# FoX attention moved from the mixer stage to the Strassen pairs, with GLA and HGRN2 side by side

## The chip, the cores and the metric

The kernel runs on one core of one Trainium2 chip. The metric is device time in microseconds (us). Before the change three runs took 2003.84, 2007.07 and 2007.81 us; their median is 2007.07 us. TensorE (PE) multiplies matrices, VectorE (DVE), ScalarE (ACT) and GpSimd (POOL) work element by element, and SyncE (SP) issues most DMAs.

## The reference

One layer of a hybrid decoder, for a prompt of 1024 tokens and for 8 samples of 4 tokens, with the same weights; width 1024, float32. Three mixers stand beside each other and are fed by one input projection:

```
def _mixer(xn, ...):
    z = xn @ w_in
    (gq, gk, gv, glr, gr, fq, fk, fv, ff, hq, hf, hi, hg, ga, gb, gc) = jnp.split(z, ...)
    o_a, gla_s = _gated_linear_scan(gq * GLA_DK ** -0.5, gk, gv, log_a, gla_s0)      # GLA, 4 heads, 64 x 128
    o_a = _rms_norm(o_a, gla_norm_g) * silu(gr)
    logf = log_sigmoid(ff + fox_bf)
    o_b = fox_attend(fq, fk, fv, logf)                                              # FoX, 4 heads of 128
    o_c, hg_s = _gated_linear_scan(silu(hq), one_minus_f, hi, log_f, hg_s0)         # HGRN2, 4 heads, 128 x 128
    o_c = _rms_norm(o_c, hg_norm_g) * silu(hg)
    merged = sigmoid(ga) * (o_a @ w_branch_a) + sigmoid(gb) * (o_b @ w_branch_b) + sigmoid(gc) * (o_c @ w_branch_c)
    return merged @ w_out, gla_s, hg_s, fk_h, fv_h, logf
# FoX, one block of 128 queries of the prompt; c = cumsum(logf)
    s = einsum('bqhd,bkhd->bhqk', qi, k) * scale
    p = softmax(where(kpos <= qpos, s + c[t] - c[s], -inf));  o = p @ v
# FoX of the samples reads 1024 past tokens through a page table, and the 4 new ones
# layer: x = x + mixer;  h = rms_norm(x);  x = x + (silu(h @ w_gate) * (h @ w_up)) @ w_down;  final rms_norm
```

## The kernel before

**Numbers and tiles.** Activations lie feature by feature: a tile has 128 features on the partitions and 1056 columns, the 1024 prompt tokens and the 32 sample tokens. Each float32 operand is split into a high and a low part (`split`, L210: ACT writes the high part, DVE subtracts it), and a product is three matmuls: high by high, high by low, low by high. An ordinary tile of a projection (`gemm`, L115) goes in three chunks of 352 columns; a chunk of the input projection is 8 x 3 matmuls (L136).

**Strassen pairs.** Most of the input projection goes in 22 pairs of output tiles (`in_pairs` L550, `pair_run` L1662). A pair is seven Strassen products (P1, P5, P6, P2, P7, P3, P4), each for two column parts of 264, each with 4 x 3 matmuls (L1693): 168 matmuls. A result is added to an output tile by DVE (L1700) or copied there by ACT (L1702). The seven weight operands are four blocks of the loaded weights and sums of them: `pair_sums` (L1625) computes the sums on DVE, `pair_split` splits each. The weights of the next pair are prepared while the last four products of this pair run; a ring of four buffers of two operands each holds them. At a pair's end `post` (L561) multiplies both outputs by the norm's factor, one on DVE, one on GpSimd (L568), applies the gates' sigmoid where there is one, and sends the tiles to DRAM.

**Mixer stage.** From 535 to 1110 us run 16 single tiles of the branch gates and the branch products (24 jobs). Between chunks, `gemm` calls `pump`, which takes one step of a generator from each of several queues: `bg` holds the four FoX heads, `bg2` FoX's sample part, `bg3` the two GLA pairs and then the four HGRN2 heads, `bgs` the sample parts of the scans. The generators issue their own matmuls among those of the tiles, in the order in which the pump meets them, and every engine runs its instructions in that order. PSUM has eight banks: seven for the pairs; in the mixer stage three for tiles (`pg`) and five for the generators (`pm`).

**FoX.** `fox_head` (L722) sums the forget gates (the scan L1146), turns the values to token order (L707), and then goes through eight query blocks: scores (L780), a DVE reduction that subtracts the bias and takes the maximum, the exponential on ACT, the normalisation on DVE (L800), transposes of the weights on PE (L746), their copy out on ACT (L748) and the product with the values (L759). Transposes and products of a block come two blocks behind its scores (`DEPTH` is 2). `fox_sample` (L811) reads 64 pages of keys and values, 0.5 MB each, with matmuls of four columns of samples (L927).

**Scans and branches.** Each scan of GLA and HGRN2 is in two halves: L1068 to L1072 scale on DVE and POOL, L1085 scores, L1106 states, L1132 and L1134 outputs. After the first eight branch tiles `any_range` (L1350) reads whether a gate's range was too wide for the fast form; the branch (L1354) with the slow form is not taken here. The branch products come in the order GLA, HGRN2, FoX.

Of the kernel before, what the change touches and what calls it, by code (L numbers as in the profile page):

```python
# [18 lines left out]
NP = 1024  # L19
# [18 lines left out]
NA, NBU, NH, NAT = 10, 8, 8, 4  # L38
KVRING = 3
LAST = ((0, 400), (400, 800), (800, NT))  # L40
SAMPLE_WITH = 2
AHEAD = 7
DEPTH = 2
# [47 lines left out]
class Body:  # L91
    def __init__(self, nc, tc, A, O):
        self.nc, self.tc, self.A, self.O = nc, tc, A, O
        self.bg, self.bgs, self.bg2, self.bg3 = [], [], [], []
# [20 lines left out]
    def gemm(self, job, nxt):  # L115
# [13 lines left out]
        for c in range(0 if job.tiles_first else NCW):  # L129
# [14 lines left out]
            self.pump(self.bg3, self.bgs, self.bg, self.bg2)  # L144
# [43 lines left out]
    def pump(self, *qs):  # L188

        if self.cold:  # L190
            return
        for q in qs or (self.bg, self.bgs, self.bg2, self.bg3):
            if q and next(q[0], "end") == "end":
                q.pop(0)
# [76 lines left out]
    def run(self):  # L271
# [21 lines left out]
        self.st = [pe.tile([128, 512], F32, name=f"st{i}") for i in range(3)]  # L293
# [5 lines left out]
    def all_jobs(self):  # L299
# [7 lines left out]
        yield Job(None, 0, None, None, run=self.in_pairs, ahead=lambda: self.pair_ahead(lambda n: self.A["winp"][n], len(PAIRS) // 2))  # L307
# [4 lines left out]
    def phase_m(self):  # L312
# [15 lines left out]
        self.bg += [self.fox_head(h) for h in range(4) if ("fv", h) not in TILES[4:]]  # L328
        self.bg3 += [self.gla_pair(p) for p in range(2)] + [self.hgrn_head(h) for h in range(4)]
# [9 lines left out]
    def constants(self):  # L339
# [21 lines left out]
        self.cmask = const("cmask", [128, 128])  # L361
        self.nmask = const("nmask", [128, NS])
        self.bmask = const("bmask", [128, NB, NS])
        self.tmask = const("tmask", [NS, NB])
        self.pts = const("pt", [1, NB * NPG], I32)
        self.ptr = const("ptr", [128, NPG], I32)
        self.hcol = const("hcol", [128, 1])
# [4 lines left out]

        self.fox_q1 = cp.tile([128, 4, NS], F32, name="fox_q1")
        self.fox_ks = cp.tile([128, 4, NS], F32, name="fox_ks")
        self.fox_vs = cp.tile([NS, 4, 128], F32, name="fox_vs")
        self.fox_cn = cp.tile([128, NS], F32, name="fox_cn")
# [173 lines left out]
    def in_pairs(self, job, nxt):  # L550
# [4 lines left out]
        def phase():  # L555
            self.close("s")
            p = self.open("p", "right", reuse_waits="tile")
            self.u = Slots(p, 6, [128, NT], F32, "pu")
            return [(p.tile([128, 1024], F32R, name=f"rh{i}"), p.tile([128, 1024], F32R, name=f"rl{i}")) for i in range(2)]

        def post(n, y):  # L561
            name = PAIRS[2 * n][0]
            e = nc.vector, nc.gpsimd
            for i in range(2):
                if name == "gq":
                    nc.vector.scalar_tensor_tensor(y[i], y[i], 0.125, self.r1, ALU.mult, ALU.mult)
                else:
                    e[i].tensor_tensor(y[i], y[i], self.r1, ALU.mult)  # L568
            if name in ("gr", "hq", "hg"):
                g = [self.u.get(), self.u.get()]  # L570
                for i in range(2):
                    self.sig = nc.scalar.activation(g[i], y[i], AF.Sigmoid)
                for i in range(2):
                    e[i].tensor_tensor(y[i], y[i], g[i], ALU.mult)
                self.u.put(*g)
            for i in range(2):
                self.keep(*PAIRS[2 * n + i], y[i])
            self.u.put(*y)

        def hook(n, k):  # L580
# [3 lines left out]
            if k == 0:  # L584
# [3 lines left out]
            elif k == 2:  # L588
# [5 lines left out]
        self.pair_run(nxt, phase, post, hook)  # L594
# [38 lines left out]
    def mixer_jobs(self):  # L633
        for n, h in TILES[4:]:
            yield self.store(n, h, (lambda h=h: self.bg.append(self.fox_head(h))) if n == "fv" else None)
# [63 lines left out]
    def tok_major(self, vT, vs):  # L699

        nc = self.nc
        v = self.u.get()
# [18 lines left out]

    def fox_head(self, h):  # L722
        nc = self.nc
        yield from self.room(5)
        vT, q, k = [self.fetch(n, h) for n in ("fv", "fq", "fk")]
        cb = self.u.get()
        nc.sync.dma_start(cb, self.lf_dram[h:h + 1, :].to_broadcast([128, NT]))
        yield
        v, vu = self.tok_major(vT, None)
        self.u.put(vT)  # L730

        self.sums(cb, NP)
        yield
        if h == SAMPLE_WITH:
            self.bg2.append(self.fox_sample())
        yield from self.room(4)
        o = self.u.get()
        psos = {}

        def turned(i, x):  # L740

            for j0 in range(0, i + 1, 4):
                nb = min(4, i + 1 - j0)
                pt = self.pm.get()
                for j in range(nb):
                    nc.tensor.transpose(pt[:, j * 128:(j + 1) * 128], x[:, (j0 + j) * 128:(j0 + j + 1) * 128], self.ident)  # L746
                P = self.hf.get()
                nc.scalar.activation(P[:, :nb * 128], pt[:, :nb * 128], AF.Copy)  # L748
                self.pm.put(pt)
                if j0 + nb == i + 1:  # L750
                    self.u.put(x)
                yield j0, nb, P

        def values(i, j0, nb, P):
            if i % 4 == 0 and j0 == 0:
                psos[0] = self.pm.get()
            pso = psos[0]
            for j in range(nb):
                nc.tensor.matmul(pso[:, (i % 4) * 128:(i % 4 + 1) * 128], v[:, j0 + j, :], P[:, j * 128:(j + 1) * 128],  # L759
                                 start=j0 + j == 0, stop=j0 + j == i)  # L760
            self.hf.put(P)
            if i % 4 == 3 and j0 + nb == i + 1:
                nc.vector.tensor_copy(o[:, (i - 3) * 128:(i + 1) * 128], pso)
                self.pm.put(pso)

        prev = []
        for i in range(8):
            n = (i + 1) * 128
            x = self.u.get()
            cbd = self.sp.tile([128, 128], F32, tag="cbd", name="cbd", bufs=2)  # L770
            nc.gpsimd.tensor_tensor(cbd, cb[:, n - 128:n], self.cmask, ALU.add)
            m = self.sp.tile([128, 4], F32, tag="fm", name="fm", bufs=4)
            init = -3.0e38
            nm = 0
            tp = turned(*prev.pop(0)) if len(prev) == DEPTH else iter(())
            for s0 in range(0, n, 512):
                part = next(tp, None)
                w = min(512, n - s0)
                ps = self.pm.get()
                nc.tensor.matmul(ps[:, :w], q[:, i * 128:(i + 1) * 128], k[:, s0:s0 + w], start=True, stop=True)  # L780
                d0 = i * 128 - s0
                full = w if d0 >= w else d0
                if full > 0:
                    nc.vector.tensor_tensor_reduce(x[:, s0:s0 + full], ps[:, :full], cb[:, s0:s0 + full], 1.0, init,
                                                   ALU.subtract, ALU.max, m[:, nm:nm + 1])
                    init = m[:, nm:nm + 1]
                    nm += 1
                if d0 < w:
# [1298 lines left out]
```

## Time and profile before

| | |
|---|---|
| median of 3 runs | 2007.07 us |
| profiled execution | 2003.84 us |
| its span | 2002.0 us |
| PE busy | 1936.3 us, 97% |
| DVE busy | 1372.3 us, 69% |
| ACT busy | 808.6 us, 40% |
| POOL busy | 456.6 us, 23% |

The span is the profiled execution from its first to its last instruction. The stages stand one behind the other: norm and first tiles to 90 us, pairs of the input projection to 535 us, mixers and branches to 1110 us, output projection to 1280 us, the FFN's pairs behind it. The granted clock in the profile's rows is a share of TensorE's full clock: 1.00 is its level of 2.4 GHz, 0.50 that of 1.2 GHz. The profile's matmul rows are pipelined: the cost of one in a row of many is the distance of the starts, not its own duration.

### The profile page before, as it was taken

The page shows a single profiled execution, that of the slowest core. Times are in us where ns is not written, and L with a number is a line of the kernel's source. Part 1 is how long each engine was busy: PE and PEld are TensorE (multiplying, and loading weights), DVE is VectorE, ACT ScalarE, POOL GpSimd, SP SyncE. Part 2 cuts the span into 40 slices and gives each one's busy share as a digit, 9 for nine tenths or more (in the row PEclk, how much of TensorE's full clock was granted, in tenths as well). Part 3 has the DMA queues.
Part 4 walks back from the last instruction along what each step waited for, and adds up shares of the span by engine and source line. Part 5 has one row for each costly group of instructions (what it writes and reads, how often), then busy time and mean ns, then how long its engine had stood idle before and what let it go on. Part 6 is the DMA issues. An engine that isn't in the chain of part 4 may idle for free. (4 is left out here: it accounts for less than half of the span.)

```text
span 2002.0 us, 36377 instructions
## 1 busy us (share of the span) xinstructions
PE 1936.3 (97%) x14590; PEld 1816.3 (91%) x14590; DVE 1372.3 (69%) x2279; ACT 808.6 (40%) x1448; POOL 456.6 (23%) x269
## 2 busy tenths in 40 slices
PE   8899999999989999999999999999999999999997
PEld 6899999999976777787788999999999999999996
DVE  8866577666476767667744555878777777667965
ACT  5433343333244435355343333543333333323435
POOL 5110122211121322112201631133222322111004
PEclk9999999999988989999999999999999999999999
DMA  3343222333434226676775443221222122333212
GB/s 132 108 158 132 99 106 97 107 107 119 135 139 152 96 98 217 213 225 220 231 252 198 160 156 119 75 75 67 101 80 75 65 83 75 133 113 121 84 59 87
DMA packets 88630, 253.65 MB, mean 127 GB/s; under 512 B 13634, under 2 KB 18690, under 8 KB 88450
## 3 DMA queue, kind: packets, MB, share of 16 engines
q1 hardware_dynamic: 86898, 250.02, 36.8%
q8 instruction: 117, 1.92, 0.4%
q10 hardware_dynamic: 1296, 0.67, 0.1%
q14 instruction: 63, 0.52, 0.1%
q0 software_dynamic: 256, 0.52, 0.1%
HBM read 183.80 MB, written 67.37 MB: 125 GB/s over the span
## 5 line engine op out<-in xcount | busy, mean ns | idle before, releaser
L136 PE MATMUL pg<-x,wh 128*128 128x352 f32 x1692 | 434.0, 336 | 11.5 <-DVE ub L629 6.7
L136 PEld LDWEIGHTS pg<-x,wh 128*128 128x128 f32 x1692 | 298.1, 192 | 37.0 <-issue 26.2
L1693 PE MATMUL pg<-x,wh 128*128 128x264 f32 x1632 | 308.6, 285 | 3.4 <-DVE du L1700 2.3
L136 PE MATMUL pg<-x,wl 128*128 128x352 f32 x846 | 280.6, 332 | 0.1
L1693 PE MATMUL pg<-x,rh 128*128 128x264 f32 x1424 | 267.3, 285 | 2.2 <-DVE fu L1700 2.2
L1693 PEld LDWEIGHTS pg<-x,wh 128*128 128x128 f32 x1632 | 253.3, 188 | 5.7 <-DVE du L1700 2.5
L1693 PE MATMUL pg<-x,wl 128*128 128x264 f32 x816 | 231.7, 284 | 2.3 <-DVE wl L215 2.3
L1693 PEld LDWEIGHTS pg<-x,rh 128*128 128x128 f32 x1424 | 221.7, 189 | 2.5 <-DVE fu L1700 2.4
L1693 PE MATMUL pg<-x,rl 128*128 128x264 f32 x712 | 202.8, 285 | 0.0
L136 PEld LDWEIGHTS pg<-x,wl 128*128 128x128 f32 x846 | 162.4, 192 | 4.2 <-issue 3.0
L1693 PEld LDWEIGHTS pg<-x,wl 128*128 128x128 f32 x816 | 153.4, 188 | 2.5 <-DVE wl L215 2.5
L568 POOL TENSOR_TENSOR pu<-pu,r 128x1056 f32<-128x1056 f32 x21 | 59.2, 2818 | 378.6 <-ACT pu L1702 378.6
L1693 PEld LDWEIGHTS pg<-x,rl 128*128 128x128 f32 x712 | 134.6, 189 | 0.0
L214 ACT ACTIVATE wh<-wf 128x512 fp32r<-128x512 f32 (+2 forms) x110 | 68.1, 619 | 158.9 <-PE pg L1693 120.2
L215 DVE TENSOR_TENSOR wl<-wf,wh 128x512 fp32r<-128x512 f32 (+2 forms) x110 | 85.6, 778 | 46.7 <-ACT wh L214 45.2
L1728 POOL TENSOR_TENSOR fu<-fu,r 128x1056 f32<-128x1056 f32 x22 | 67.2, 3057 | 215.9 <-ACT fu L1702 202.7
L107 ACT ACTIVATE wh<-wf 128x1024 fp32r<-128x1024 f32 (+2 forms) x60 | 51.3, 854 | 146.8 <-PE pg L136 105.8
L1630 DVE TENSOR_TENSOR st<-wf 128x512 f32<-128x512 f32 x44 | 87.2, 1982 | 32.8 <-DMA wf<-in_winp 19.0
L1693 PE MATMUL pg<-pr,wh 128*128 128x264 f32 x544 | 103.1, 288 | 3.7 <-ACT pu L1702 3.7
L1700 DVE TENSOR_TENSOR pu<-pu,pg 128x264 f32<-128x264 f32 x132 | 56.4, 428 | 72.2 <-PE pg L1693 71.9
L215 DVE TENSOR_TENSOR rl<-wf,rh 128x512 fp32r<-128x512 f32 x85 | 69.8, 822 | 47.7 <-ACT rh L214 46.8
L214 ACT ACTIVATE rh<-wf 128x512 fp32r<-128x512 f32 x85 | 53.5, 631 | 112.2 <-PE pg L1693 83.7
(519 smaller groups left out, 4594.6 us busy)
## 6 DMA issues: line engine op xcount, KB each, us to landing
z_dram<-pu SPq DMA_DIRECT2D x44, 528.0 KB
wf<-in_winp SPq DMA_DIRECT2D x44, 512.0 KB
wf<-in_wgu SPq DMA_DIRECT2D x44, 512.0 KB
u<-z_dram SPq DMA_DIRECT2D x36, 528.0 KB
ub<-z_dram SPq DMA_DIRECT2D x28, 528.0 KB
wf<-in_win SPq DMA_DIRECT2D x19, 512.0 KB
a_dram<-fu SPq DMA_DIRECT2D x18, 528.0 KB
du<-a_dram SPq DMA_DIRECT2D x14, 528.0 KB
```

The costliest lines, as they stand in the source:

```text
L107: nc.scalar.activation(wh[:, :n], wf[:, :n], AF.Copy)
L136: nc.tensor.matmul(ps[:m, :CW], a[:, k, :], b[:, sl], start=n == 0, stop=n == 3 * job.kt - 1)
L214: nc.scalar.activation(h, x, AF.Copy)
L215: (eng or nc.vector).tensor_tensor(l, x, h.bitcast(F32), ALU.subtract)
L568: e[i].tensor_tensor(y[i], y[i], self.r1, ALU.mult)
L1630: nc.vector.tensor_tensor(s[0], a2[:, x], a2[:, y], ALU.add)
L1693: nc.tensor.matmul(ps, a[:, w], b, start=first and m == 0, stop=m == 3 * K - 1, skip_group_check=not first)
L1700: nc.vector.tensor_tensor(out, out, ps, ALU.add)
L1728: TT = lambda e, o, x, y, op=ALU.mult: e.tensor_tensor(o, x, y, op)
```

## The change

**FoX goes to the pairs.** `in_pairs` opens FoX's own buffers (`fox_open`) once the norm's are closed; PSUM is split into six banks for the pairs and two for FoX. After each product of a column part, that is after every 12 matmuls, `pair_run` calls `beside`, which takes one step of the queue `bg`: first the four heads, then the sample. `fox_head` is written anew as 33 steps with a fixed order: in a step of the blocks with more than 512 keys stand a score matmul of one block and the transposes or value products of the block before. `fox_sample` gives way twice per page instead of once. A head joins the queue when its value tile is stored.

**Weights of the pairs roll.** In place of a whole pair of weights ahead, a table (`ROLL`) says which split and which sum is done behind each product; three raw buffers turn, five quarters of split weights are held instead of eight. `post` becomes a generator that is advanced one step behind each product. The order of the pairs changes: the tiles with a sigmoid come last.

**GLA beside HGRN2.** Two queues, `bg3` for the two GLA pairs and `bg4` for the four HGRN2 heads, are both pumped between the gate tiles. In a scan the second half's first matmuls are issued later, among the first half's.

**Branches.** Their order is FoX, GLA, HGRN2. The slow form, not taken, now saves and restores the partial result.

```
-NA, NBU, NH, NAT = 10, 8, 8, 4
+NA, NBU, NH, NAT = 10, 8, 10, 4
-PAIRS += [(n, t) for n, c in (("gq", 2), ("gk", 2), ("gv", 4), ("gr", 4), ("hq", 4), ("hf", 4), ("hg", 4), ("hi", 4)) for t in range(c)]
-PAIRS += GATES[24 - 2 * NGP:]
+PAIRS += [(n, t) for n, c in (("gq", 2), ("gk", 2), ("gv", 4), ("hf", 4), ("hi", 4)) for t in range(c)]
+PAIRS += GATES[24 - 2 * NGP:20]
+PAIRS += [(n, t) for n in ("gr", "hq", "hg") for t in range(4)]
+PAIRS += GATES[20:]
...
                 if k == 3 and job.kt == KD:
-                    self.pump(self.bg, self.bg3, self.bgs, self.bg2)
+                    self.pump(self.bg3, self.bgs)
...
-            self.pump(self.bg3, self.bgs, self.bg, self.bg2)
+            self.pump(self.bg4, self.bgs, *(() if job.kt == KD else (self.bg3,)))
...
-            self.u = Slots(p, 6, [128, NT], F32, "pu")
-            return [(p.tile([128, 1024], F32R, name=f"rh{i}"), p.tile([128, 1024], F32R, name=f"rl{i}")) for i in range(2)]
+            self.u = Slots(p, 5, [128, NT], F32, "pu")
+            ring = p.tile([128, 512], F32R, name="rh"), p.tile([128, 512], F32R, name="rl")
+            self.fox_open(p)
+            self.bg.append(self.fox_head(0))
+            return [ring]
...
-        self.pair_run(nxt, phase, post, hook)
+        self.pair_run(nxt, phase, post, hook, beside=lambda: self.pump(self.bg))
+        self.drain(self.bg)
...
+    def fox_open(self, p):
+        self.fa = Slots(p, 5, [128, NT], F32, "fa")
+        self.fp = Slots(p, 3, [128, 512], F32, "fp")
+        self.fb = Slots(p, 6, [128, 128], F32, "fb")
+        self.fs = Slots(p, 4, [128, 8], F32, "fs")
...
+        for i in range(9):
+            S = list(blocks[i][0]) if i < 8 else []
+            TV = list(blocks[i - 1][2]) if i else []
+            steps = max(len(S), len(TV))
+            if i < 8 and steps == len(S):
+                steps += 1
+            for j in range(steps):
+                if stored:
+                    stored.pop(0)()
+                if pend:
+                    pend[0]()
+                if TV and j % 2:
+                    TV.pop(0)()
+                if S:
+                    S.pop(0)()
+                    new = None if S else blocks[i][1]
+                else:
+                    new = None
+                if TV and j % 2 == 0:
+                    TV.pop(0)()
+                if pend:
+                    pend[1]()
+                pend = new
                 yield
...
-        order = [(bi, f) for bi in (0, 2, 1) for f in range(8)]
+        order = [(bi, f) for bi in (1, 0, 2) for f in range(8)]
...
+    ROLL = {3: (1, "P1", "S1"), 4: (1, "P5", "S2"), 5: (1, "P6", "S3"), 6: (1, "P2", "S4"), 0: (0, "P7"), 1: (0, "P3"), 2: (0, "P4")}
...
-        self.banks(7)
+        self.banks(6 if beside else 7)
...
+                    if beside:
+                        beside()
                 has.add(self.READS[name])
+                if pend and next(pend[0], "end") == "end":
+                    pend.pop()
+                if rolling:
+                    m, *names = self.ROLL[k]
+                    self.roll(n + m, *names)
```

In `fox_head` the pair `pend` holds the exponential and the normalisation of a block; `S` are its scores, `TV` the transposes and value products of the block before.

On PE before, in the mixer stage, FoX's transposes (L746), value products (L759) and scores (L780) stand a few tile matmuls (L136) apart:

```order
L780 MATMUL pg_97<-ub_5427,ub_5421 128x256
L136 MATMUL pg_98<-x_75,wh_71 128x352
L136 MATMUL pg_98<-x_76,wh_71 128x352
L746 MATMUL pg_94<-c_ident,ub_5426 128x128 x4
...
L136 MATMUL pg_98<-x_79,wh_71 128x352
L759 MATMUL pg_91<-h_5407,u_5398 128x128 x4
...
L746 MATMUL pg_95<-c_ident,ub_5422 128x128 x4
L780 MATMUL pg_94<-ub_5427,ub_5421 128x512
L759 MATMUL pg_96<-h_5412,u_5398 128x128 x4
```

On PE of the change, in the pairs, a step of FoX (scores L801, transposes L832, value products L845) stands behind every 12 pair matmuls (L1813), and FoX's tiles have two banks in turn, here `pg_93` and `pg_94`:

```order
L801 MATMUL pg_94<-fa_825,fb_830 128x512
L832 MATMUL pg_93<-f_ident,fa_824 128x128 x4
L1813 MATMUL pg_96<-x_77,wh_71 128x264
...
L845 MATMUL pg_94<-fp_827,fa_822 128x128 x4
L801 MATMUL pg_93<-fa_825,fb_830 128x256
L1813 MATMUL pg_97<-x_77,wh_71 128x264
...
L832 MATMUL pg_93<-f_ident,fa_824 128x128
L1813 MATMUL pg_98<-pr_219,wh_72 128x264
...
L845 MATMUL pg_94<-fp_828,fa_822 128x128
```

The FoX matmuls stand now at even distances, and the scores' second part takes the bank that the transposes have just left.

On DVE before, in a pair, stand the evacuations (L1700), the splits (L215), the post product (L568) and the sums (L1630, L1631):

```order
L215 TENSOR_TENSOR rl_821<-st_237,rh_820 128x512
L1700 TENSOR_TENSOR pu_818<-pu_818,pg_92 128x264
L1700 TENSOR_TENSOR pu_818<-pu_818,pg_96 128x264
L215 TENSOR_TENSOR rl_821<-wf_70,rh_820 128x512
L568 TENSOR_TENSOR pu_818<-pu_818,r_261 128x1056
L1630 TENSOR_TENSOR st_235<-wf_70 128x512
L1631 TENSOR_TENSOR st_236<-st_235,wf_69 128x512
```

On DVE of the change, in a pair, FoX's reductions (L806), their scaling (L813, L823) and the normalisation (L824) stand between the splits (L215) and the sums (L1753, L1757):

```order
L824 TENSOR_SCALAR fa_822<-fa_822,fs_835 128x640
L215 TENSOR_TENSOR wl_74<-wf_69,wh_72 128x512
L806 ISA fa_825,fs_836<-pg_93,fa_821 128x512
L806 ISA fa_825,fs_836<-pg_94,fa_821,fs_836 128x128
L1753 TENSOR_TENSOR st<-wf_69 128x512
L806 ISA fa_825,fs_836<-pg_94,fb_832,fs_836 128x128
...
L1757 TENSOR_TENSOR wf_69<-raw_236,wf_69 128x512
L813 TENSOR_SCALAR fs_836<-fs_836 128x1
L215 TENSOR_TENSOR wl_74<-wf_70,wh_72 128x512
...
L824 TENSOR_SCALAR fa_825<-fa_825,fs_836 128x768
```

A sum of weights, which can wait for its DMA, now stands ahead of a reduction that empties a FoX bank.

## Rows read from the trace of the kernel before

**Rows 1.** The page: busy time, share of the span and instructions of each engine.

```profile
PE 1936.3 (97%) x14590; PEld 1816.3 (91%) x14590; DVE 1372.3 (69%) x2279; ACT 808.6 (40%) x1448; POOL 456.6 (23%) x269
```

**Rows 2.** Windows, start:end, length, busy us (instructions) by engine, clock, DMA share, GB/s.

```profile
100.00:500.00 400.00, 400.00 (x3290) 399.97 (x3289) 262.13 (x362) 150.88 (x310) 70.87 (x25) 1.00 0.33 116
545.00:1110.00 565.00, 539.48 (x3990) 434.89 (x3989) 361.83 (x888) 246.83 (x443) 108.98 (x90) 0.96 0.56 187
545.00:735.00 190.00, 177.25 (x1118) 138.98 (x1117) 124.69 (x355) 79.52 (x163) 37.70 (x40) 0.89 0.35 119
735.00:1060.00 325.00, 316.06 (x2596) 250.75 (x2594) 211.14 (x492) 145.91 (x258) 61.40 (x41) 0.99 0.68 222
```

**Rows 3.** PE's waits, 545 to 1110 us: line, releaser: total us, times, longest.

```profile
PE pg L136 <- DVE ub L629: 6.7, 2, 5.2
PE pg L136 <- DVEq L1354: 3.8, 1, 3.8
PE pg L746 <- DVE ub L800: 3.5, 2, 2.8
PE pg L780 <- DVE ub L230: 3.1, 1, 3.1
PE pg L707 <- DVE u L908: 2.3, 1, 2.3
PE pg L746 <- DVE fs L797: 1.8, 2, 1.7
...
```

**Rows 4.** Windows of the seven stretches at clock 0.50, some, and their sum.

```profile
562.18:569.01 6.83, 3.64 (x12) 3.62 (x13) 6.55 (x14) 2.44 (x4) 5.12 (x6) 0.50 0.28 111
...
640.69:654.34 13.65, 13.65 (x42) 10.52 (x41) 11.47 (x37) 3.88 (x9) 3.81 (x4) 0.50 0.55 204
712.37:722.61 10.24, 10.24 (x38) 7.99 (x39) 1.58 (x4) 3.31 (x7) 0.00 (x0) 0.50 0.15 59
920.58:924.00 3.42, 3.42 (x35) 1.82 (x34) 2.47 (x12) 3.36 (x8) 1.51 (x2) 0.50 0.41 149
...
sum 47.79, PE 44.30 PEld 34.60 DVE 26.54 ACT 17.24 POOL 10.45; mean PE 6.33 PEld 4.94 DVE 3.79 ACT 2.46 POOL 1.49
```

**Rows 5.** PE's timeline, 704 to 715 us: start, us, engine, line, operation, count.

```profile
704.84 0.49 PE L1132 MATMUL pg<-at,ub 128*128 128x128 f32 x2
...
705.67 0.71 PE L1132 MATMUL pg<-at,u 128*128 128x128 f32 x4
...
713.34 0.79 PE L1134 MATMUL pg<-h,h 64*128 64x128 f32 x2
...
714.79 0.79 PE L1134 MATMUL pg<-h,h 64*128 64x128 f32 x2
```

**Rows 6.** DVE's timeline, 558 to 566 us.

```profile
559.00 2.28 DVE L1146 TENSOR_TENSOR_SCAN u<-one,u 128x1024 f32<-128x1024 f32 x1
```

**Rows 7.** DVE's timeline, 635 to 640 us; in brackets the idle time before.

```profile
635.59 3.78 DVE L1146 TENSOR_TENSOR_SCAN u<-one,u 128x1024 f32<-128x1024 f32 x1 [1.01 <-DMA u<-lf_dram]
```

**Rows 8.** Line L1700: durations in ns min/median/max, first and last start, forms.

```profile
L1700 DVE TENSOR_TENSOR pu<-pu,pg x132: 412/429/430, 95.7 to 531.9; 128x264 f32<-128x264 f32 x132
```

**Rows 9.** Lines L1630, L568 and L800, in the same form.

```profile
L1630 DVE TENSOR_TENSOR st<-wf x44: 674/1990/2971, 77.0 to 1693.5; 128x512 f32<-128x512 f32 x44
L568 POOL TENSOR_TENSOR pu<-pu,r x21: 2457/2701/3262, 106.5 to 536.1; 128x1056 f32<-128x1056 f32 x21
L800 DVE TENSOR_SCALAR ub<-ub,fs x17: 278/553/2484, 572.3 to 854.6; 128x128 f32<-128x128 f32 x3, 128x1024 f32<-128x1024 f32 x3, 128x256 f32<-128x256 f32 x2, 128x512 f32<-128x512 f32 x2
```

**Rows 10.** All of PE's waits, 70 to 545 us.

```profile
PE pg L1693 <- ACT pu L1702: 3.7, 1, 3.7
PE pg L1693 <- DVE wl L215: 2.3, 1, 2.3
```

**Rows 11.** PE's timeline, 1006 to 1008 us, a page step of the sample.

```profile
1007.24 0.62 PE L927 MATMUL pg<-ub,ub 128*4 128x128 f32 x16
```

**Rows 12.** DVE's waits, 100 to 500 us, that on the weights' DMA.

```profile
DVE st L1630 <- DMA wf<-in_winp: 19.0, 16, 2.4
```

More of the change, by code (lines that the diff above doesn't have):

```diff
@@ L292, in run @@
         pe, s = self.open("pe", "right"), self.open("s", "right")
[L293 removed]
+        self.st = [pe.tile([128, 512], F32, name="st")]
+        self.raw3 = pe.tile([128, 1024], F32, name="raw3")
         self.u = Slots(s, 12, [128, NT], F32, "su")
@@ L766, in fox_head @@
[L766 to L788, printed above, removed]
-                    nc.vector.tensor_tensor_reduce(x[:, n - 128:n], ps[:, d0:w], cbd, 1.0, init,
-                                                   ALU.subtract, ALU.max, m[:, nm:nm + 1])
-                    init = m[:, nm:nm + 1]
-                    nm += 1
-                self.pm.put(ps)
-                if part:
-                    values(i - DEPTH, *part)
-            sm = self.sp.tile([128, 4], F32, tag="fs", name="fs", bufs=4)
-            nc.vector.tensor_scalar(sm[:, 0:1], m[:, nm - 1:nm], -1.0 / RT128, None, ALU.mult)
-            nc.scalar.activation(x[:, :n], x[:, :n], AF.Exp, bias=sm[:, 0:1], scale=1.0 / RT128, accum_out=sm[:, 1:2])
-            nc.vector.reciprocal(sm[:, 2:3], sm[:, 1:2])
-            nc.vector.tensor_scalar(x[:, :n], x[:, :n], sm[:, 2:3], None, ALU.mult)
-            prev.append((i, x))
-            yield
@@ L807, in fox_head @@
                 yield
-        nc.sync.dma_start(self.o_dram[4 + h][:, 0:NP], o[:, 0:NP])
-        self.u.put(q, k, vu, cb, o)
+        while stored:
+            stored.pop(0)()
+        self.fa.put(k, cb, v)
     def fox_sample(self):
-        nc, A, sp = self.nc, self.A, self.sp
-        yield from self.room(6)
-        fox_v = sp.tile([128, 4, NS], F32, name="fox_v")
+        nc, A = self.nc, self.A
+        q1, ks, fv, small = [self.fb.get() for _ in range(4)]
+        fox_q1, fox_ks, fox_v = [t.rearrange("p (h t) -> p h t", t=NS) for t in (q1, ks, fv)]
@@ L865, in fox_sample @@
         order += [("vc", b, 2 * s2) for b in range(NB) for s2 in range(4)]
-        yield from self.room(KVRING - 1)
-        ring = [self.wf.get()] + [self.u.get() for _ in range(KVRING - 1)]
+        ring = [self.fa.get() for _ in range(KVRING)]
         sent = []
@@ new lines, in pair_run @@
+    def pair_run(self, nxt, phase, post, hook, into=None, beside=None):
+        nc, K, rolling = self.nc, self.K, self.rolling
+        self.ring.append((self.wh.get(), self.wl.get()))
+        if rolling:
+            self.roll(0, "P6", "S3", "P2", "S4")
+            self.ring += phase()
+        else:
+            self.pair_split(2)
+            self.pair_split(3)
+            self.ring += phase()
+            for n in (4, 5, 6):
+                self.pair_split(n)
+            self.pair_load(1)
+        self.banks(6 if beside else 7)
+        pend = []
@@ L1673, in pair_run @@
         for n in range(self.pairs):
             last = n == self.pairs - 1
-            if last:
+            if last and not rolling:
                 self.wf.put(*self.raw)
@@ L1714, in pair_run @@
                                 nxt = None
-                elif k >= 3:
+                elif k >= 3 and not rolling:
                     if k < 5:
@@ L1723, in pair_run @@
             if post:
-                post(n, y)
+                assert not pend
+                steps = post(n, y)
+                if steps is not None:
+                    next(steps)
+                    pend.append(steps)
+        for steps in pend:
+            for _ in steps:
+                pass
+        self.rolling = False
     def ffn_up(self, job, nxt):
```

382 lines of the change are left out of this document (238 added, 144 removed).

## The prediction

> **What bounds the kernel now.** I read the page's busy times first: TensorE (PE) is busy 97% of the span [rows 1]. A kernel in that state gets faster in two ways only, by less PE work or by less PE time that is lost. The first doesn't happen here: the changed program holds the same matmuls of every shape on the path that runs (the 288 fewer of 128x352 stand in the branch for wide ranges, which is not taken). So the question is where PE loses time, and the windows by stage answer it [rows 2]. In the stretch of Strassen pairs (100 to 500 us) PE is busy all 400 us, has the full clock of 2.4 GHz, and starts 3290 matmuls of 264 columns: 121.6 ns each, with no gap. Behind it lies the mixer stage, 545 to 1110 us: PE is busy 539.5 of 565 us, so it idles 25.5 us, and its granted clock is 0.96, 0.89 in the first 190 us. This stage is the only large one with something to win, and FoX, GLA and HGRN2 all stand in it.
>
> Next the waits of PE in that stage [rows 3]. FoX's own matmuls (L746, L759, L780, and L707 for the sample) wait 3.5 + 3.1 + 2.3 + 1.8 us, and 1.8 us in four smaller groups, together 12.5 us. Tile matmuls wait 6.7 us for a late evacuation (L629) and 3.8 us for the branch (L1354). The rest, 2.3 us, belongs to the scans.
>
> Then the clock. Seven stretches of the stage run at 1.2 GHz, 47.8 us in all [rows 4]. What such a microsecond costs is read where the same code stands at both levels [rows 5]: one L1132 and one L1134 take 0.83 us at the high level (704.84 to 705.67) and 1.45 us at the low one (713.34 to 714.79). So 0.43 of each low microsecond is lost, 20.5 us in all. What PE did before each fall: at 562 us and 640 us it had just waited 5.2 us and 3.1 us; at 920 us it had waited 2.3 us; before 712 us it had run some 8 us of small GLA matmuls without one tile matmul between them.
>
> **The change, part by part.** The sum is made against the profiled execution: 2003.84 us, of which 2002.0 us are span. The median of the runs is 2007.07 us, 3.2 us above, and the forecast is set on the median.
>
> *Taken out of the mixer stage.* (a) FoX's 12.5 us of waits leave with its matmuls. (b) The 6.7 us at L629: the long one, 5.2 us, ends when VectorE (DVE) gets through a burst in which a FoX scan of 1024 columns takes 2.3 us and GLA's first steps the rest [rows 6]. The scan goes, HGRN's gate (four DVE passes over 1056 columns) comes, so I take half, 3.3 us, and keep 0 and 6.7 as ends. (c) The low stretches that begin behind a FoX wait, at 640 us (13.65 us) and 920 us (3.42 us): the first follows a scan of FoX's bias that took 3.78 us [rows 7]. 17.1 us x 0.43 = 7.3 us. The other five (30.7 us) come from GLA's clump, the stage's start and the branch, and stay. Sum of (a) to (c): 12.5 + 3.3 + 7.3 = 23.1 us.
>
> *Put beside the pairs.* Four heads of 33 steps each, one step after every 12 pair matmuls (12 x 121.6 ns = 1.46 us); 14 steps to a pair, so the heads last 132 / 14 = 9.4 pairs. A reader of a step's result now stands at least one such group behind it, mostly two or three. Lower end of the new waits: 0, as 400 us of pairs show no wait behind equally spaced results. Upper end: FoX has two PSUM banks here (five before). A block of more than 512 keys has two places where the next bank is due about as soon as DVE can have emptied it: 1.46 us of pair matmuls cover a reduction of up to three instructions. One foreign DVE evacuation of 0.43 us in front [rows 8] then shows on PE. 32 blocks x 2 x 0.43 = 27.5 us. To that come long DVE operations. DVE's sum L1630 takes 0.67 us at best and 1.99 us in the median, 2.97 us at most, while the GpSimd product L568 runs 2.7 us in each pair [rows 9]. A FoX normalisation (L800) shows the same, 2.48 us against a median of 0.55 us [rows 9]. At 2.3 us once a pair, 9.4 x 2.3 = 21.6 us. Upper end 49 us. Between 0 and the 12.5 us that the same matmuls waited for where they stood closer, I take the middle, 6 us.
>
> The Trainium skill says of this in "SBUF — State Buffer", section "Who interferes with whom", that VectorE and GpSimd share one pair of ports as an exclusive lock, and that the second to come is blocked for the other's whole instruction; an operation with two SBUF inputs and a normalisation from SBUF to SBUF are among those that can want it. By that rule each pair would hold FoX up once while GpSimd multiplies, 21.6 us in place of my 6, and the time would be about 2006 us. The trace agrees that such operations stretch to the length of the GpSimd operation [rows 9], but in the pairs no PE wait came of it [rows 10].
>
> *The sample.* Its 64 page steps keep their form: 16 records of 4-column matmuls, then full ones; the one at 1007.24 us lasts 0.62 us [rows 11]. That is paid beside the pairs as before: 0. Its pages are 33.5 MB; with 24 pair matmuls to a step (2.9 us and 0.6 us of its own) they flow at about 150 GB/s beside the pairs' 116 GB/s, DMA share 0.33 [rows 2]. Before, the sample's stretch ran at 222 GB/s and 0.68 [rows 2], so it fits. Should a weight part come late, DVE waits in front of its first sum; before, L1630 did so 16 times, 2.4 us at most [rows 12]. Eleven pairs with the sample: 0 to 26 us; I take 0, since none of those waits reached PE.
>
> *The rolling schedule.* Splits (seven a pair) and sums (four) are the same instructions, each now issued three to four products (9 to 12 us) ahead instead of up to seven. At 0.8 us a split the cover is ample: 0. The start of the pairs waited 3.7 + 2.3 us [rows 10] and does the same sums in the same order: 0, from -6 to +4 us.
>
> *GLA beside HGRN.* Both now go at once, without FoX between. The 20 or so tile matmuls among the first 250 scan matmuls can't hide a chain, but two chains fill each other: 0, with ends from -13.2 us (30.7 low microseconds x 0.43 all gone) to +17 us (40 us more of them). FoX's branch first: same loads and splits, 0.
>
> Sum: -23.1 + 6 = -17 us, 1987 us for the profiled execution, 1990 us as a median.
>
> **The rivals.**
> A, slower. The two banks and DVE's queue hold up FoX's steps among the pairs, at the upper end of 49 us: -23.1 + 49 = +26, 2033 us. It decides from 23.1 / 132 = 0.175 us of wait per step. For it: DVE is already busy 262 of 400 us in the pairs [rows 2], and FoX's reductions and normalisations come on top; it is a queue in order, so a sum that waits for its weights holds FoX's evacuation too. Against it: DVE's long operations brought no PE wait among the pairs so far [rows 10].
>
> B, a larger gain. With no FoX, nothing starves the tile matmuls and the clock holds in GLA's part also: another 13.2 + 3.4 us, and no waits beside the pairs: -23.1 - 16.6 = -40, 1967 us. For it: the pairs run at full clock throughout. Against it: before 712 us the clock fell behind GLA's matmuls alone, and these stand as close as ever.
>
> C, waits change places. GLA and HGRN together starve the tile matmuls as FoX and GLA did, so that (b) and (c) come to nothing, and FoX waits 9 us among the pairs: -12.5 + 9 = -3.5, 2003.6 us, within what can be told from no change. For it: the first 70 us of the new stage hold even fewer tile matmuls.
>
> **How the numbers follow.** The forecast has 0.38 (its own range 1979 to 2002), A 0.25, B 0.23, C 0.14. A's cases start where the waits pass 23 us, so they reach down to 2011. Faster or slower means by over 0.2%, 4 us, which a measurement of this kernel can tell from no change. Faster: 0.37 of the forecast, B, and a few of C's, 0.64; same 0.11; slower 0.25. The range for 8 in 10 takes in B and A: from 1957 (B with the start's 6 us and some sample cover more) to 2036 us.
>
> **What would show it.** Right: in the pairs' stretch, now some 570 us long, waits of PE for FoX's transposes (L832) and products (L801, L845) of 3 to 12 us together, and full clock; in the mixer stage, some 430 us, no wait over 4 us but the branch, and 25 to 35 us at the low level. A would show as many waits of 0.2 to 1 us on L801, L832 and L845, released by DVE L806, L824 or ACT. B shows as two low stretches or fewer. C shows as tile matmuls that wait at L640, and low stretches as long as before. The forecast is wrong as a whole if pair matmuls (L1813) wait for their weights, or if DVE is busy over 90% in the heads' part.

## The result and the profile after

The changed kernel takes 2011.01 us in the median of 20 runs, the kernel before 2002.92 us in the median of its 20: a ratio of 1.0052 (95% interval 1.0033 to 1.0071). By the ratio it is slower by about 10 us (the medians lie 8.1 us apart), where 0.8% faster was forecast. The profiled execution took 2009.41 us, its span is 2007.6 us.

The page of the changed kernel, busy times, answers to [rows 1]:

```profile
PE 1938.9 (97%) x14590; PEld 1821.8 (91%) x14590; DVE 1366.0 (68%) x2267; ACT 820.4 (41%) x1485; POOL 451.7 (22%) x271
```

The number of matmuls is the same, and PE's share too. Where the time went shows in the windows of the two stages, from the first pair matmul of the input projection to the last, and from there to the first pair matmul of the FFN (columns as in [rows 2]). First the kernel before:

```profile
75.60:534.40 458.80, 452.82 (x3697) 452.17 (x3696) 294.33 (x416) 169.39 (x347) 73.55 (x27) 0.99 0.33 115
534.40:1273.70 739.30, 713.21 (x5063) 608.33 (x5062) 461.02 (x1014) 312.23 (x517) 175.18 (x142) 0.97 0.52 174
```

And the changed one:

```profile
75.50:681.70 606.20, 593.60 (x5118) 541.67 (x5118) 368.05 (x691) 236.54 (x513) 102.77 (x71) 1.00 0.49 160
681.70:1278.90 597.20, 576.20 (x3642) 526.78 (x3641) 378.83 (x724) 258.48 (x391) 144.59 (x101) 0.95 0.40 139
```

The pairs grew by 147.4 us and the mixer stage shrank by 142.1 us: 5.3 us lost. PE's idle time (length less busy) is 12.6 us in the pairs where it was 6.0, and 21.0 us in the mixer stage where it was 26.1. The clock of the mixer stage fell from 0.97 to 0.95. All that follows is as long as before.

PE's waits in the mixer stage of the changed kernel, the largest of them, against [rows 3]:

```profile
PE pg L1372 <- DVE skq L1249: 9.0, 3, 4.7
PE pg L136 <- ACTq L1441: 3.2, 1, 3.2
PE pg L1372 <- DVE at L1176: 2.7, 1, 2.7
PE pg L1429 <- DVE rg_m L1426: 2.1, 1, 2.1
```

FoX's waits are gone, and new ones have come: L1372 are the first matmuls of a scan's sample part (L1285 before), which did not wait in the kernel before and wait 12.3 us now. Where the clock is low in this stage, some windows and the sum, against [rows 4]:

```profile
725.60:729.00 3.40, 3.13 (x22) 2.71 (x23) 2.72 (x12) 1.70 (x3) 0.60 (x2) 0.50 0.00 0
766.60:776.80 10.20, 10.20 (x22) 4.94 (x22) 2.42 (x4) 1.55 (x2) 0.00 (x0) 0.50 0.14 56
814.30:821.10 6.80, 6.14 (x42) 4.92 (x46) 6.44 (x16) 0.83 (x2) 1.74 (x2) 0.50 0.25 79
855.30:862.10 6.80, 5.04 (x21) 3.92 (x21) 4.92 (x14) 1.62 (x3) 0.00 (x0) 0.50 0.00 0
...
sum 54.40, PE 51.27 PEld 39.09 DVE 29.16 ACT 16.87 POOL 4.42; mean PE 5.70 PEld 4.34 DVE 3.24 ACT 1.87 POOL 0.49
```

Three of the four, 17.0 us, begin during waits of L1372 (3.5 us to 725.9, 4.7 us to 815.0, 2.7 us to 857.1 us); the second, 10.2 us, follows 10 us of scan matmuls with no tile matmul among them and no wait. Of the five that are not shown, three (13.6 us) begin during or just behind other waits, and two (13.6 us) follow no wait. The low level holds 54.4 us, 6.6 us more than before.

In the pairs, PE's waits between 95 and 650 us are all FoX's, at the full clock:

```profile
PE pg L832 <- DVE fa L824: 4.0, 4, 1.3
PE pg L832 <- DVE fs L806: 2.8, 2, 1.5
PE pg L1027 <- DVE fa L1020: 1.7, 1, 1.7
PE pg L845 <- DVE fs L806: 1.1, 1, 1.1
```

### The profile page after: what moved, and what is told of

The parts are those of the page before. It is cut to its first block, busy times and chain, and to the rows that moved or that the text cites. A ratio compares the mean times of both kernels' runs of the same rounds, so it can differ in the third digit from the quotient of the medians.

```text
span 2007.6 us, 36645 instructions
## 1 busy us (share of the span) xinstructions
PE 1938.9 (97%) x14590; PEld 1821.8 (91%) x14590; DVE 1366.0 (68%) x2267; ACT 820.4 (41%) x1485; POOL 451.7 (22%) x271
## 5 line engine op out<-in xcount | busy, mean ns | idle before, releaser
L136 PE MATMUL pg<-x,wh 128*128 128x352 f32 x1692 | 425.8, 332 | 5.2 <-ACTq L1441 3.2
L1813 PE MATMUL pg<-x,wh 128*128 128x264 f32 x2080 | 401.5, 288 | 7.1 <-POOL frmul L754 2.6
L1813 PEld LDWEIGHTS pg<-x,wh 128*128 128x128 f32 x2080 | 322.8, 188 | 19.9 <-issue 9.6
L136 PEld LDWEIGHTS pg<-x,wh 128*128 128x128 f32 x1692 | 300.6, 192 | 13.3 <-issue 4.3
L1813 PE MATMUL pg<-x,wl 128*128 128x264 f32 x1040 | 295.6, 284 | 0.4 <-DVE wl L215 0.4
L136 PE MATMUL pg<-x,wl 128*128 128x352 f32 x846 | 278.4, 329 | 0.0
L1813 PEld LDWEIGHTS pg<-x,wl 128*128 128x128 f32 x1040 | 195.7, 188 | 0.6 <-DVE wl L215 0.6
L1813 PE MATMUL pg<-x,rh 128*128 128x264 f32 x976 | 187.6, 288 | 2.8 <-DVE fu L1820 2.8
L1813 PE MATMUL pg<-pr,wh 128*128 128x264 f32 x832 | 164.5, 294 | 0.1
L136 PEld LDWEIGHTS pg<-x,wl 128*128 128x128 f32 x846 | 162.7, 192 | 0.0
L1813 PEld LDWEIGHTS pg<-x,rh 128*128 128x128 f32 x976 | 152.2, 189 | 6.3 <-DVE fu L1820 3.2
L215 DVE TENSOR_TENSOR wl<-wf,wh 128x512 fp32r<-128x512 f32 (+2 forms) x125 | 109.7, 880 | 54.0 <-ACT wh L214 43.1
L1813 PE MATMUL pg<-x,rl 128*128 128x264 f32 x488 | 139.3, 285 | 0.0
L1813 PEld LDWEIGHTS pg<-pr,wh 128*128 128x128 f32 x832 | 130.0, 190 | 9.5 <-issue 5.6
L1813 PE MATMUL pg<-pr,wl 128*128 128x264 f32 x416 | 119.0, 286 | 0.0
L1822 ACT ACTIVATE pu<-pg 128x264 f32<-128x264 f32 x176 | 66.6, 381 | 67.7 <-PE pg L1813 60.1
L1813 PEld LDWEIGHTS pg<-x,rl 128*128 128x128 f32 x488 | 92.3, 189 | 0.0
```

What stands on the lines that cost most here:

```text
L215: (eng or nc.vector).tensor_tensor(l, x, h.bitcast(F32), ALU.subtract)
L1813: nc.tensor.matmul(ps, a[:, w], b, start=first and m == 0, stop=m == 3 * K - 1, skip_group_check=not first)
L1822: nc.scalar.activation(out, ps, AF.Copy)
```

## The experiments

Theory M: the scans, not FoX, make PE wait in the mixer stage, so what FoX took with it came back. Theory P: FoX costs more among the pairs than it did among the mixers.

**FoX left out of either kernel.** The branch product reads FoX's value tiles in its place.

```
-        self.pair_run(nxt, phase, post, hook, beside=lambda: self.pump(self.bg))     # after
-        self.drain(self.bg)
+        self.pair_run(nxt, phase, post, hook, beside=lambda: None)
+        self.bg.clear()
...
-        self.bg += [self.fox_head(h) for h in range(4) if ("fv", h) not in TILES[4:]]     # before
```

> The changed kernel with FoX's attention left out (heads and sample; the branch product reads the value tiles in its place). Theory P, the price in the pairs: a FoX step among pair matmuls costs more than its own matmuls, since about 177 groups each slow the switch by 0.1 us or more and 9.6 us of waits come to it. By the trace FoX holds 130.7 us beside the pairs, and the pair matmuls next to it 20 us more than their spacing: the time falls by 151 us, to about 1860. Theory M, the mixer stage lost what it should have won (17 us of scan waits, 54 us at the low clock, FoX in the pairs at its own price): it falls by 131 us only, to about 1880, and the mixer stage still shows about 17 us of scan waits and 54 us at the low clock.

> The kernel before with FoX's attention left out in the same way. If FoX costs as much in the mixer stage as in the pairs, it falls as far as e1 does, by 131 to 151 us, to about 1852 to 1872. Theory P: it falls by 8 to 20 us less than e1 does, for FoX was cheaper there. Theory M: without FoX the scans of the kernel before starve too, so new waits of PE for scan steps of 10 us or more appear in the mixer stage, and the fall is smaller than FoX's own matmuls (some 120 us).

The changed kernel falls to 1865.1 us (0.9314 of before, 0.9285 to 0.9343), the kernel before to 1864.9 us (0.9306, 0.9283 to 0.9328). Without FoX the two can't be told apart, within some 7 us: rolling weights, the two queues and the order of the branches are worth nothing together. By the ratios FoX's price is 148 us in the pairs and 139 us in the mixer stage. That is the direction of theory P, but the intervals together leave about 8 us to either side of the 9 us between the two. The waits in the mixer stage speak for theory M: those of the kernel before without FoX, the largest of them,

```profile
PE pg L1286 <- DVE skq L1163: 16.2, 10, 4.6
PE pg L136 <- DVEq L1355: 3.7, 1, 3.7
PE pg L136 <- DVE u L630: 3.1, 1, 3.1
```

and the windows of its mixer stage, and of the changed kernel's without FoX:

```profile
533.20:1125.00 591.80, 561.18 (x3643) 518.20 (x3641) 379.90 (x724) 257.09 (x390) 150.55 (x101) 0.97 0.41 140
```

```profile
75.40:535.00 459.60, 451.47 (x3697) 450.00 (x3697) 275.15 (x413) 171.03 (x350) 78.88 (x30) 1.00 0.34 117
535.00:1132.60 597.60, 576.48 (x3643) 527.60 (x3641) 380.70 (x724) 259.13 (x391) 145.31 (x101) 0.95 0.40 139
```

Take FoX away, and PE idles 30.6 us in that stage, not the 13.6 us that 26.1 less FoX's 12.5 would leave. The scans wait at L1286 in FoX's stead. The changed kernel's mixer stage is as long without FoX in the pairs (597.6 us) as with it (597.2 us). The stages of the two kernels without FoX are not to be set against each other: the execution of the kernel before took 1853.9 us at a mean clock of 0.985, 11 us less than its median.

**The sample left out, the heads kept,** to price both parts in both places.

```
-                    if h == 3:                               # after
-                        self.bg.append(self.fox_sample())
...
-        if h == SAMPLE_WITH:                                 # before
-            self.bg2.append(self.fox_sample())
```

> The changed kernel with FoX's sample left out and its heads kept (the sample columns of the branch product read the values in their place). By the trace the sample holds 53 us beside the pairs (steps of 0.76 and 0.74 us, 64 of them, and what stands around them), so it falls to about 1958. Theory S (each of the sample's page steps pays its own switch in the pairs, and shared it with other work in half of the cases before): the sample's price here is 8 to 12 us above that in the kernel before, and the heads cost the same in both. Theory H (the heads' waits on two banks and on VectorE's queue make the difference): the sample costs the same in both, within 3 us.

> The kernel before with FoX's sample left out in the same way. Theory S: it falls by 41 to 45 us only, to about 1960. Theory H: it falls as far as the changed kernel does, by some 53 us, to 1950.

The changed kernel falls to 1956.8 us (0.9779, 0.9759 to 0.9799), the kernel before to 1942.4 us (0.9703, 0.9680 to 0.9726). In hundredths of the time of before, the heads cost 4.65 among the pairs (0.9779 - 0.9314) and 3.97 among the mixers (0.9703 - 0.9306), 93 and 80 us; the sample 2.73 and 2.97, 55 and 59 us. So theory S is wrong: the sample is no dearer in the pairs. The heads are, by 14 us (the four intervals together leave about 10 us to either side). Why, the windows tell: the pairs of the changed kernel without the sample (its execution took 1968.7 us, 12 us above the median, with a mixer stage at a clock of 0.93; its pairs alone are read), and the mixer stage of the kernel before without it,

```profile
75.80:632.30 556.50, 540.29 (x4257) 519.58 (x4256) 349.63 (x657) 228.57 (x502) 97.22 (x62) 1.00 0.33 111
```

```profile
533.50:1213.40 679.90, 650.76 (x4202) 585.04 (x4201) 439.81 (x980) 308.53 (x510) 162.03 (x133) 0.98 0.40 138
```

against the same stages without FoX. The heads add 88.8 us of busy PE to the pairs (540.29 - 451.47) and 89.6 us to the mixers (650.76 - 561.18): the same work, as near as clocks of 0.97 and 0.98 in the mixers let one say. But to the pairs they add 8.1 us of idle PE (16.2 - 8.1), and to the mixers none (29.1 against 30.6): there they wait too, and fill as much of the scans' waits. What was 16.2 us at L1286 is with the heads

```profile
PE pg L1285 <- DVE skq L1162: 2.5, 3, 1.8
```

By these windows the heads cost 96.9 us in the pairs and 88.1 us in the mixers, and the sample 49.7 us in the pairs (606.20 - 556.50) and 59.4 us in the mixers (739.30 - 679.90). PE's waits in the pairs without the sample show what it is worth there:

```profile
PE pg L1813 <- DVE pu L1820: 6.1, 5, 2.1
PE pg L832 <- DVE fa L824: 3.9, 4, 1.3
...
PE pg L832 <- DVE fs L806: 1.5, 2, 1.1
PE pg L845 <- DVE fs L806: 1.1, 1, 1.1
```

The heads' own waits are 6.5 us. The 6.1 us are pair matmuls that wait for evacuations, in the last pairs, when the heads are done; without any FoX they are 4.5 us, and in the changed kernel, whose sample runs there, they are gone. So FoX as a whole adds only 4.5 us of idle PE to the pairs (12.6 - 8.1): the sample covers the pairs there, as the heads covered the scans. Theory H named the right part of FoX and half of the cause: the heads' waits in the pairs are real, but they had as many before. What is missing is the cover that they gave the scans.

**The page steps, halved and doubled.** What a step costs was measured by itself.

```
                                          kt[:, :, h, :], ...)      # each page step in two halves (e7)
+                        if h == 1:
+                            yield
                     yield
-                    yield
...
                                          kt[:, :, h, :], ...)      # two page steps in one place (e6)
-                    yield
-                    yield
+                    if qq:
+                        for _ in range(4):
+                            yield
```

The same was done to the value pages.

> The changed kernel with two of the sample's page steps in one place and four pumps behind them, in place of one and two: 32 switches between pair matmuls and FoX fewer, at the same rate of pages. If the switch is what FoX pays more for in the pairs (by the trace 0.1 us on the first pair matmul behind a step, and 0.09 us on the last before it), it is 32 x 0.19 = 6 us faster, 2005. If the price is in the matmuls themselves, 2011. Two pages fall due at once on three buffers: should they come late, waits of PE for the DMA show it, and the time is above 2011.

> The changed kernel with each of the sample's 64 page steps cut in two halves, one pump apart: 64 switches more, the same matmuls, the same rate of pages. If a switch costs 0.19 us, 12 us slower, 2023; if it costs nothing, 2011.

Halved steps: 2044.7 us (1.0225, 1.0194 to 1.0257), 34 us above the change in place of 12. Two in one place: 2007.8 us (1.0021, 0.9996 to 1.0045). Here a key page's step (L978) stands among pair matmuls on PE's timeline of the changed kernel, of two steps in one place, and of the half step:

```profile
430.32 0.29 PE L1813 MATMUL pg<-pr,wl 128*128 128x264 f32 x1
430.53 0.64 PE L978 MATMUL pg<-fa,fa 128*32 128x256 f32 x8
...
431.45 0.28 PE L1813 MATMUL pg<-x,rl 128*128 128x264 f32 x1
```

```profile
432.19 0.28 PE L1815 MATMUL pg<-x,rl 128*128 128x264 f32 x1
432.40 1.07 PE L978 MATMUL pg<-fa,fa 128*32 128x256 f32 x16
...
433.75 0.28 PE L1815 MATMUL pg<-x,wl 128*128 128x264 f32 x1
```

```profile
440.20 0.28 PE L1815 MATMUL pg<-x,rl 128*128 128x264 f32 x1
440.41 0.63 PE L978 MATMUL pg<-fa,fa 128*32 128x256 f32 x4
...
441.32 0.29 PE L1815 MATMUL pg<-x,rl 128*128 128x264 f32 x1
```

From the first row to the last stand three pair matmuls, 3 x 121.6 ns; the rest is the step: 0.76 us, 1.19 us for two, 0.75 us for a half. A key step's place costs 2 x 0.76 - 1.19 = 0.33 us. And two heads' matmuls take as long as four, as if the four 32-column products ran at the same time: 32 more halves of key pages are 32 x 0.75 = 24 of the 34 us, and no measure of a switch. (Half of the 64 steps are of key pages; the value pages' steps were not measured in this way.) The pairs' stretch with two steps in one place is 598.1 us, 8.1 less than 606.2, though PE waits 2.0 us there for the pages' DMA.

**GLA and HGRN2 one behind the other.** With the new order of the scan's steps, then with that of the kernel before:

```
-        self.bg3 += [self.gla_pair(p) for p in range(2)]
-        self.bg4 += [self.hgrn_head(h) for h in range(4)]
+        self.bg3 += [self.gla_pair(p) for p in range(2)] + [self.hgrn_head(h) for h in range(4)]
...
-            self.pump(self.bg4, self.bgs, *(() if job.kt == KD else (self.bg3,)))
+            self.pump(self.bg3, self.bgs)
```

> The changed kernel with GLA and HGRN2 one behind the other in one queue, pumped twice a chunk as before, in place of side by side. If two chains at once are what makes VectorE late for PE (theory M), the scan waits of 17 us fall below 8 us and the time to about 2000. If two chains fill each other's gaps, as I had it in the forecast, it is slower than the change, 2015 to 2030.

> GLA and HGRN2 in one queue (as in the run before that was slower than the change) and the steps of a scan in the order of the kernel before, where both halves' factors are made one step earlier. In that run PE waited 3.6, 6.0 and 5.0 us for scores of a scan's second product (L1180). If the new order of the steps makes these waits, they go: 2006 to 2012. If one chain alone starves PE in either order, 2018 to 2024.

In series with the new order: 2021.3 us (1.0082, 1.0069 to 1.0095), slower than the change; with the old order 2009.3 us (1.0030, 0.9998 to 1.0062), as fast as the change. In series with the new order PE waits at the transposes of a scan's key factors (L1180), which stand too close behind GpSimd's product that makes them (L1157),

```profile
PE pg L1180 <- POOL h L1157: 16.9, 5, 6.0
PE pg L1371 <- DVE skq L1248: 3.6, 3, 2.4
```

and in the old order for the sample's factors:

```profile
PE pg L1371 <- DVE skq L1248: 15.0, 8, 4.9
PE pg L1378 <- DVE skh L1363: 4.1, 2, 2.1
```

Two queues and the new order mend each other, and end where one queue and the old order stood.

**More cover for the scans' sample part,** in the changed kernel and in the one before:

```
         nc.vector.tensor_tensor(kh, kh, k[:, ss], ALU.mult)
-        yield
-        yield
+        for _ in range(6):
+            yield
```

> The changed kernel with six steps in place of two between the scans' sample factors and the matmuls that read them (and one more 512-column buffer). Leaving FoX out changed both kernels alike in the mixer stage, so its waits belong to the scans. If they are a cover that is too short, the waits of PE at L1372 (12.3 us) fall below 4 us, and the low stretches that begin there shrink: 5 to 15 us faster than the change, 1996 to 2006. If PE waits there only because VectorE is behind as a whole, the waits move on to other scan steps: 2008 to 2014.

> The kernel before with six steps of cover at the same place (L1278), and nothing else. In it PE waits only 0.7 us there, since FoX's matmuls stand between. If that cover is what FoX gave the scans, nothing changes: 2000 to 2005. If a longer cover helps whatever stands there, it falls by some 10 us to 1993.

The changed kernel needs one more buffer of 512 columns for this; two more do not fit in the on-chip memory. The change with more cover: 1999.6 us (0.9986, 0.9971 to 1.0002), 11 us less. The kernel before: 2007.0 us (1.0025, 1.0003 to 1.0047), a little slower. The mixer stage of the first:

```profile
680.00:1266.10 586.10, 561.40 (x3643) 519.90 (x3641) 376.94 (x724) 264.35 (x395) 144.33 (x101) 0.97 0.41 142
```

PE idles no less there (24.7 us against 21.0): other waits came, 3.0 us at the range test and 4.4 us at the branch, the scans' at most 2.4 us. But the clock is 0.97, not 0.95, and PE is busy 14.8 us less for the same matmuls. By these windows the gain is all in the clock. The execution they show took 6 us less than the median, but the other runs agree: read at the same mean clock, this kernel and the change take the same time, as the table in the section behind this one shows. In the kernel before the longer chain came out at its end, at the branch,

```profile
PE pg L136 <- DVEq L1354: 15.6, 1, 15.6
```

and the windows of its mixer stage show 14.1 us more of idle PE (40.2 against 26.1) and 8.5 us less of busy PE:

```profile
533.80:1278.70 744.90, 704.67 (x5064) 602.75 (x5062) 459.04 (x1014) 328.44 (x529) 172.55 (x142) 0.97 0.52 172
```

**Both edits together.** Six steps of cover and pages two by two; the same with one queue and the old order of the scan; ten steps of cover.

> The changed kernel with both edits that shortened it: six steps of cover for the scans' sample factors, and the sample's page steps two by two. The two act in different stages. If they add, 11 + 3 us (by the runs) to 11 + 8 us (by the pairs' stretch alone, 598.1 us against 606.2) below the change: 1992 to 1997, faster than the kernel before. If the mixer stage's gain depends on when it starts, about 2000.

> The same two edits, with GLA and HGRN2 in one queue and the steps of a scan as in the kernel before. With a short cover this form waited 4.9, 4.5 and 2.4 us at the scans' samples (L1371), so a longer cover should give as much here as beside two queues: 1990 to 1996. If one chain alone leaves PE without work, it ends 5 to 10 us above the run with two queues.

> As the run with both edits, but ten steps of cover in place of six. The six steps left single waits of up to 3 us at the scans' scores, which stand behind VectorE's queue and not behind this cover: no change against six steps, within 3 us.

They add: 1991.2 us (0.9938, 0.9918 to 0.9959), with one queue 1995.7 us (0.9988, 0.9961 to 1.0015), with ten steps 1987.5 us (0.9921, 0.9892 to 0.9950). The first and the last beat both kernels; the one with one queue can't be told from the kernel before. Ten steps came out 3.7 us below six, where no change within 3 us was expected, but the two intervals overlap. The windows of the first:

```profile
75.50:673.40 597.90, 583.92 (x5117) 542.84 (x5116) 363.81 (x691) 233.55 (x511) 104.78 (x71) 1.00 0.49 162
673.40:1258.20 584.80, 559.36 (x3642) 518.32 (x3641) 378.08 (x724) 264.55 (x395) 143.31 (x101) 0.98 0.41 142
```

## Why the prediction was wrong

The step that failed is "Taken out of the mixer stage", the 23.1 us of (a) to (c).

- **(a) and (b), the waits, 15.8 us.** FoX's waits left, as said. I let nothing take their place. With FoX out of the kernel before, the scans alone waited as long; in the changed kernel the stage's idle time fell by 5.1 us only. A wait of PE in a stage where several chains take turns belongs to the stage: FoX's matmuls were late at some places, and at others they were the work that let the scans' factors become ready.
- **(c), the clock, 17.1 low microseconds less.** It went the other way, 54.4 us in place of 47.8. I gave each low stretch to the chain that waited in front of it. The scans' new waits of 2.7 to 4.7 us each brought one, 17.0 us in all, and 23.8 us followed no wait at all. In the execution of the kernel before without FoX that is shown above, the low level holds 30.7 us of the stage, as (c) had it; but three of its six runs show a mean clock of 0.970 to 0.972, below any of the kernel before, so no run shows that FoX was what held the clock down.
- **Beside the pairs, 6 us of waits.** Right in its sum: 9.6 us of FoX's, within the 3 to 12 that were to show, at the full clock, and the start of the pairs gained 3.4 us, so that their idle time grew by 6.6 us. Partly that was luck: I had not forecast that the sample would cover some 5 us of waits that the pairs have without FoX. The reductions that free a bank (L806) cost 3.9 us, the normalisations (L824) 4.0 us; rival A's 49 us did not come. That bound was too high as a sum, too: of the 32 blocks only 16 have more than 512 keys, so 13.8 us in place of 27.5 and 35 in place of 49. Of the lock of VectorE and GpSimd that the Trainium skill describes ("SBUF — State Buffer", "Who interferes with whom"), by which the second to come is blocked for the other's whole instruction, the trace shows two clear cases: a normalisation took up to 2165 ns with a median of 584 ns.

```profile
L824 DVE TENSOR_SCALAR fa<-fa,fs x32: 274/584/2165, 99.2 to 364.8; 128x128 f32<-128x128 f32 x4, 128x256 f32<-128x256 f32 x4, 128x384 f32<-128x384 f32 x4, 128x512 f32<-128x512 f32 x4
```

The longest, at 318 us, and the GpSimd product and the PE wait beside it:

```profile
317.51 2.65 POOL L573 TENSOR_TENSOR pu<-pu,r 128x1056 f32<-128x1056 f32 x1 [4.89 <-ACT pu L1822]
318.15 2.17 DVE L824 TENSOR_SCALAR fa<-fa,fs 128x256 f32<-128x256 f32 x1
320.46 0.41 PE L832 MATMUL pg<-f_ident,fa 128*128 128x128 f32 x2 [1.31 <-DVE fa L824]
```

It ended 0.2 us behind the GpSimd product; the other three of 256 columns took 0.35 us. One of 512 columns, at 109 us, took 2.10 us in place of 0.48 and cost PE 0.92 us. So 2.2 of the 4.0 us are such meetings, two in 32 normalisations, where the 21.6 us had counted one in each pair.

- **The sample at no charge.** Right: 53.3 us of busy PE in the pairs (593.60 - 540.29), and its price is not higher there. But its form I had half right: 32 of the 64 page steps, the key pages', are eight products of 32 columns and not 16 of 4.
- **The rolling schedule and GLA beside HGRN2 at 0.** Right as a sum, within some 7 us, shown by the two kernels without FoX.

In the prediction's own terms, then: -5.1 us for (a) and (b), +2.8 us for (c) (6.6 x 0.43) and +6.6 us beside the pairs make +4.3 of the 5.3 us that the two stages lost, where -17 was forecast.

Rival B's clock did not come: it needed FoX to be what starves PE. Rival C was the mechanism, with the scans in place of the tile matmuls as those that starve; its sign, tile matmuls that wait at L640, did not show, and its 2003.6 us still booked the 12.5 us of (a) as won. The measured time lies where A's cases begin, but A's mechanism, over 23 us of FoX's waits in the pairs, was not there.

Of the 10 us between the kernels the profiled executions, both at a mean clock of 0.979, show 5.6. The clock differs from run to run: the 20 runs of the change go from 2004.6 us at a mean clock of 0.980 to 2024.3 us at 0.969. A straight line through each kernel's runs, with one slope for all, gives 1.6 us for each 0.001 of the mean clock, with a scatter of 1.6 us about it. Read at 0.980 (estimates from these lines):

| at a mean clock of 0.980, us | before | changed |
|---|---|---|
| whole | 2003 | 2006 |
| without FoX | 1858 | 1858 |
| without the sample | 1949 | 1957 |
| with six steps of cover | 2010 | 2006 |

So at the same clock the change costs 3 us: the heads are some 8 us dearer in the pairs and the sample some 6 us cheaper. The rest of the 10 us is a lower clock: ten of the change's 20 runs show 0.969 to 0.976, while the kernel before shows 0.974 to 0.987 in the 80 runs that were timed beside the experiments. What starts the low stretches that follow no wait, as that at 766 us, was not settled.

## What to carry to other kernels

When work is moved out of a stage, don't book its waits as won: ask which chain will wait at that place without it, and, before building, run the kernel with the work left out. Idle time that one chain causes may be cover that it gives another. In a stage whose clock falls behind waits, cut the single long waits first, even if the total of the waits stays.

## What the runs showed of the hardware

- Six steps of cover made PE wait longer in sum (24.7 us for 21.0) and the stage 11 us shorter: PE was busy 561.4 us in place of 576.2 with the same matmuls, at a granted clock of 0.97 in place of 0.95.
- Key pages' products of 32 columns for four heads take no longer than for two: 0.76 us and 0.75 us for the step.
- A key page's step costs 0.33 us for its place alone among pair matmuls (0.76 us for one, 1.19 us for two in one place); with all page steps two by two, 32 places fewer, the pairs were 8.1 us shorter.
- A normalisation of 256 columns that met a GpSimd product of 2.65 us took 2.17 us in place of 0.35, until just behind the product's end, and PE waited 1.3 us for it.
- At 766.6 us of the changed kernel the granted clock fell to 0.50 for 10.2 us behind 10 us of scan matmuls in which the profile shows no wait of PE.
